# Sliding windows of an image batch: the iota behind four loads, copies in the band-crossing units, and the two final stores as one transfer each

## The chip, the cores and the metric

One core of one Trainium2 chip. The metric is the device time of one execution in microseconds; a lower number is better. Where two kernels are compared they ran on the same chip in alternation, and a ratio is the mean time of one kernel's fast runs over the mean of the other's fast runs of the same rounds, so it is not quite the ratio of the medians that are quoted.

## The reference

The batch is x of 16 images, 64 channels, 64 rows, 64 columns, float32 (16.8 MB). All windows of 8 by 8 at stride 4 are cut out, 15 by 15 of them an image, with all channels:

```python
for i in range(n_h):            # 15
    for j in range(n_w):        # 15
        h_start, w_start = i * stride, j * stride
        result[:, i, j] = x[:, :, h_start:h_start + 8, w_start:w_start + 8].copy()
```

The output has 3,600 windows of 64x8x8 floats, which is 3,600 contiguous rows of 16 KB, 59.0 MB. There is no arithmetic: the kernel loads, rearranges and stores.

## The kernel before

x lies in SBUF as a tile L of 128 partitions. Partition p = 64 ch + 4 b + q holds the channel half ch, image b and row band q (16 rows). A window needs both channel halves, so VectorE and ScalarE copy pieces of L into a gather tile G, in which one partition holds one whole window, 16 KB; G is then stored. There are four buffers G, used in turn.

The loads come from three queues. SyncE and GpSimd take eight partitions at a time:

```python
SMALL, HWP = 4, 8
def load(eng, ch, y, q, c0, c1):
    p0 = ch * HP + y * QP + q
    eng.dma_start(out=L[p0 : p0 + QP - HQ + 1 : HQ, c0:c1, :, :], in_=x_v[ch, y, q, :, c0:c1, :])

nc.gpsimd.iota(pi[:, :], ...)          # then some twenty 128x1 VectorE operations make the row indices
# ... cut ...
EC = 8
nc.scalar.dma_start(out=L[HP : HP + (B - 1) * HQ + 1 : HQ, 0:EC, :, :], in_=x_b[1, 0, :, 0:EC, :])
for y in range(NY):                    # 2
    for q in range(HQ):                # 4
        load(nc.sync, 0, y, q, SMALL, CL)            # hw is true for all eight
        load(nc.gpsimd, 0, y, q, 0, SMALL)
        load(nc.gpsimd, 1, y, q, EC if q == 0 else 0, CL)
```

A "plain" unit fills G with windows that lie inside one row band; its store has 128 rows. A "crossing" unit has, in one half of the partitions, windows that straddle two bands, so half of each piece comes through a stream shuffle from the next partition. The last band has no next one: 16 of the 128 rows get an index out of bounds and are not stored (the trace has 3,600 packets of 16 KB, one for each window). In a hi unit they lie in the upper 64 partitions, in a lo unit in the lower 64.

```python
def fill(g, half, s, j, lo, n, copies):
    # ... cut: the slices d, cols, f and cs ...
    for ch in (half, 1 - half):
        copy = copies[ch != half]
        if s < NSLOT - 1:
            copy(out=g[d, cs, :, :], in_=L[f, :, s * ST : s * ST + WS, cols])
        else:
            copy(out=g[d, cs, 0:ST, :], in_=L[f, :, s * ST : RB, cols])
            nc.vector.stream_shuffle(out=g[d, cs, ST:WS, :], in_=L[f, :, 0:ST, cols], mask=nxt)

act, dve = nc.scalar.copy, nc.vector.tensor_copy
def shf(out, in_):                       # a shuffle with the identity, which copies
    nc.vector.stream_shuffle(out=out, in_=in_, mask=same)
def mix(out, in_):                       # a quarter of the channels on ScalarE, the rest a shuffle
    k = out.shape[1] // 4
    act(out=out[:, 0:k], in_=in_[:, 0:k])
    shf(out=out[:, k:], in_=in_[:, k:])

def unit(j, s, fast=False):
    g = tile_()
    if s == 0:                           # plain
        fill(g, 0, 0, j, 0, HP, (act, dve if fast else shf))
        fill(g, 1, 1, j, 0, HP, (act, dve if fast else mix))
        scatter(g, idx, j, s)            # an indirect DMA issued by GpSimd
    else:                                # crossing
        turn = crossed % 2
        crossed += 1
        fill(g, turn, s, j, 0, HP, (act, act))
        fill(g, 1 - turn, s + 1, j, 0, HP, (shf, mix))
        scatter(g, (idx_hi, idx_lo)[turn], j, s)
```

In all there are 29 indirect stores: six of a `part` stage while the loads still run, then three fast plain units among them, then five groups of three crossing units and one plain unit. The last column of windows is not stored by index:

```python
j = NW - 1
tile_()                                  # skips one buffer
for s in range(2):
    g = tile_()
    # ... two copies on ScalarE, two on VectorE, 32x2048 each ...
    for q in range(HQ):                  # eight transfers of 256 KB in all
        free((nc.sync, nc.scalar)[s * q % 2].dma_start(out=o_q[q * NSLOT + s, j], in_=g_q[QP + q : QP + q + (B - 1) * HQ + 1 : HQ]))
```

Of the kernel before, what the change touches and what calls it, by code (L numbers as in the profile page):

```python
# [10 lines left out]
def kernel(  # L11
# [7 lines left out]
    nc = tc.nc  # L19
    P = nc.NUM_PARTITIONS  # L20

    B, C, H, W = x.shape
    Bo, NH, NW, Co, WSo, WSo2 = out.shape
    WS = int(window_size)
    ST = int(stride)
# [5 lines left out]
    CH = 2  # L31
    HQ = P // (B * CH)
    CL = C // CH
    RB = H // HQ
    NSLOT = RB // ST
    NWIN = NH * NW
    CFREE = C * WS * WS
    HP = P // CH
    YB = 8
    NY = B // YB  # L40
    QP = YB * HQ
# [7 lines left out]
    L = lpool.tile([P, CL, RB, W], f32)  # L49
# [4 lines left out]
# [5 lines that stand above are left out]
# [3 lines left out]
    def itile(name):  # L62
        return ipool.tile([P, 1], i32, name=name)

    pi, tb, tq, tc_, th, idx, idx_y0, idx_y1, idx_lo, idx_hi = (
        itile(n) for n in ("pi", "tb", "tq", "tc", "th", "idx", "idx_y0", "idx_y1", "idx_lo", "idx_hi")
    )
    FAR = float(2 * B * NWIN)
    nc.gpsimd.iota(pi[:, :], pattern=[[0, 1]], base=0, channel_multiplier=1)  # L69

    def bits(d, shift, mask):
        nc.vector.tensor_scalar(out=d[:, :], in0=pi[:, :], scalar1=shift, scalar2=mask, op0=ALU.logical_shift_right, op1=ALU.bitwise_and)  # L72
# [4 lines left out]
    def tt(d, a, b, op):  # L77
        nc.vector.tensor_tensor(out=d[:, :], in0=a[:, :], in1=b[:, :], op=op)  # L78
# [20 lines left out]
    tt(idx_lo, tb, th, ALU.add)  # L99
    mul(th, tc_, NW)  # L100
    tt(idx_lo, idx_lo, th, ALU.add)


    EC = 8
    x_b = x.rearrange("b (ch cl) (hq r) w -> ch hq b cl (r w)", ch=CH, hq=HQ)
    nc.scalar.dma_start(out=L[HP : HP + (B - 1) * HQ + 1 : HQ, 0:EC, :, :], in_=x_b[1, 0, :, 0:EC, :])

    for y in range(NY):
        for q in range(HQ):
            hw = y * HQ + q < HWP  # L110
            if hw:
                load(nc.sync, 0, y, q, SMALL, CL)
            load(nc.gpsimd, 0, y, q, 0, SMALL if hw else CL)
            load(nc.gpsimd, 1, y, q, EC if q == 0 else 0, CL)

    o_v = out.rearrange("b i j c r w -> (b i j) (c r w)")
    nxt = [min(p + 1, 31) for p in range(32)]
# [3 lines left out]
    o_q = out.rearrange("b i j c r w -> i j b (c r w)")  # L121

    def free(st):
        tc.declare_no_dep(st.ins, group="stores", reason="each store writes rows of its own")
        tc.add_to_no_dep_group("stores", st.ins)

    def scatter(g, ix, j, s):
        st = nc.gpsimd.indirect_dma_start(  # L128
            out=o_v,
            out_offset=bass.IndirectOffsetOnAxis(ap=ix[:, 0:1], axis=0),  # L130
            in_=g.rearrange("p c r w -> p (c r w)"),
            in_offset=None,
            element_offset=(s * NW + j) * CFREE,
            bounds_check=B * NWIN - 1,
            oob_is_err=False,
        )
        free(st)

    def fill(g, half, s, j, lo, n, copies):

        d = slice(half * HP + lo, half * HP + lo + n)
        cols = slice(j * ST, j * ST + WS)
        for ch in (half, 1 - half):
            f = slice(ch * HP + lo, ch * HP + lo + n)
            cs = slice(ch * CL, (ch + 1) * CL)
# [8 lines that stand above are left out]
    same = list(range(32))  # L154


    def shf(out, in_):
        nc.vector.stream_shuffle(out=out, in_=in_, mask=same)  # L158

    def mix(out, in_):  # L160
        k = out.shape[1] // 4
        act(out=out[:, 0:k], in_=in_[:, 0:k])  # L162
        shf(out=out[:, k:], in_=in_[:, k:])


    EARLY = 3
# [2 lines left out]
    def tile_():  # L169
        nonlocal at  # L170
        at += 1
        return G[(at - 1) % NG]
# [16 lines left out]
    def unit(j, s, fast=False):  # L189
        nonlocal crossed  # L190
        g = tile_()
        if s == 0:
            fill(g, 0, 0, j, 0, HP, (act, dve if fast else shf))
            fill(g, 1, 1, j, 0, HP, (act, dve if fast else mix))
            scatter(g, idx, j, s)
        else:

            turn = crossed % 2
            crossed += 1
            fill(g, turn, s, j, 0, HP, (act, act))  # L200
            fill(g, 1 - turn, s + 1, j, 0, HP, (shf, mix))
            scatter(g, (idx_hi, idx_lo)[turn], j, s)

    for n in range(EARLY):
# [3 lines left out]
    for n in range(EARLY):  # L208
        part(1, 2 * n)
        unit(*plain.pop(0), fast=True)  # L210
    while plain:
        for w in cross[:3]:
            unit(*w)
        cross = cross[3:]
        unit(*plain.pop(0))


    j = NW - 1
    tile_()
    for s in range(2):  # L220
        g = tile_()
        cols = slice(j * ST, j * ST + WS)
        for y in range(NY):
            d = slice(QP + y * QP, QP + (y + 1) * QP)
            for ch, copy in enumerate((act, dve)):
                f = slice(ch * HP + y * QP, ch * HP + (y + 1) * QP)
                copy(out=g[d, ch * CL : (ch + 1) * CL, :, :], in_=L[f, :, s * ST : s * ST + WS, cols])  # L227
        g_q = g.rearrange("p c r w -> p (c r w)")
        for q in range(HQ):
            free((nc.sync, nc.scalar)[s * q % 2].dma_start(out=o_q[q * NSLOT + s, j], in_=g_q[QP + q : QP + q + (B - 1) * HQ + 1 : HQ]))  # L230


# [33 lines left out]
```

## Time and profile before

| | before |
|---|---|
| time, median | 190.28 us (190.25 to 190.29), later 190.26 to 190.66 beside other kernels |
| span of the profiled run | 189.0 us (this run took 190.74 us, some 0.5 us over the median) |
| VectorE, ScalarE busy | 142.5 us, 139.2 us |
| mean rate of all transfers | 401 GB/s |
| last indirect store issued by GpSimd | 172.51 us |
| last plain stores issued | 181.44 to 182.86 us |

The prediction below shows the lines of the page, of the windows view and of the timeline that carry this. A window line reads: from and to, length, busy us of VectorE, ScalarE and GpSimd with their instruction counts, the clock, the DMA share (the mean share of 16 DMA engines with a packet in flight; it can pass 1: it is 1.03 from 8 to 28 us, where two queues load, and 1.00 to 1.01 from 52 to 172 us, under GpSimd's stores alone) and the rate.

The view by source line of the launch code has the columns line, engine, operation, count, shortest/median/longest in ns, first start and last start in us.

```profile
L261 POOLq DRAIN  x3: 51/105/12829, 172.3 to 188.7; - x3
```

GpSimd's queue drains for 12.8 us, from 172.3 to 185.1 us; GpSimd's last store has landed 1.89 us before the drain's end, at 183.23 us. In this kernel the drain's end is over 3.8 us before the span's end.

### The profile page before, as it was taken

The page shows a single profiled execution, that of the slowest core. Times are in us where ns is not written, and L with a number is a line of the kernel's source. Part 1 is how long each engine was busy: PE and PEld are TensorE (multiplying, and loading weights), DVE is VectorE, ACT ScalarE, POOL GpSimd, SP SyncE. Part 2 cuts the span into 40 slices and gives each one's busy share as a digit, 9 for nine tenths or more (in the row PEclk, how much of TensorE's full clock was granted, in tenths as well). Part 3 has the DMA queues.
Part 4 walks back from the last instruction along what each step waited for, and adds up shares of the span by engine and source line. Part 5 has one row for each costly group of instructions (what it writes and reads, how often), then busy time and mean ns, then how long its engine had stood idle before and what let it go on. Part 6 is the DMA issues. An engine that isn't in the chain of part 4 may idle for free.

```text
span 189.0 us, 557 instructions
## 1 busy us (share of the span) xinstructions
DVE 142.5 (75%) x200; ACT 139.2 (74%) x89; POOL 46.9 (25%) x50
## 2 busy tenths in 40 slices
DVE  4000009999697979799989999999999999997410
ACT  0000009998699999988889999999999999974740
POOL 7321212207217170522220222222222222223000
DMA  4999999999999999999999999999999999999993
GB/s 118 308 409 397 402 401 397 397 403 394 427 434 420 435 434 416 434 434 413 437 437 408 439 430 420 423 437 416 427 413 434 428 409 430 406 437 378 427 389 153
DMA packets 11044, 75.81 MB, mean 401 GB/s; under 512 B 3344, under 2 KB 3344, under 8 KB 7440
## 3 DMA queue, kind: packets, MB, share of 16 engines
q0 software_dynamic: 8784, 65.81, 84.0%
q1 hardware_dynamic: 2048, 8.91, 12.0%
q10 hardware_dynamic: 208, 1.05, 1.8%
q14 instruction: 4, 0.03, 0.0%
HBM read 16.78 MB, written 62.91 MB: 422 GB/s over the span
## 4 chain that ended last, share of the span: by engine, by line
DMA 66%; DVE 18%; issue 6%; ACT 3%; POOL 2%; DVEq 0%; ACTq 0%; PEldq 0%
DMA out_dram<-G,idx_hi 24%; DMA L<-in_x_dram 23%; DMA out_dram<-G,idx 13%; DVE G L158 10%; DMA out_dram<-G,idx_y 7%; DVE G L151 5%; DVE G L181 3%; ACT G L227 2%; POOL L L58 2%; ACT G L148 1%; DVE G L148 0%; DVEq L181 0%; POOL pi L69 0%; DVEq L158 0%; PEldq L261 0%
## 5 line engine op out<-in xcount | busy, mean ns | idle before, releaser
L148 ACT COPY G<-L 64x2048 f32<-64x2048 f32 x46 | 87.2, 1896 | 5.5 <-DMA out_dram<-G,idx 2.3
L181 DVE COPY G<-L 32x2048 f32<-32x2048 f32 x30 | 36.6, 1221 | 29.3 <-DMA L<-in_x_dram 26.7
L158 DVE STREAM_SHUFFLE G<-L 64x1024 f32<-64x1024 f32 (+3 forms) x40 | 55.7, 1392 | 1.3
L151 DVE STREAM_SHUFFLE G<-L 64x1024 f32<-64x1024 f32 x30 | 38.5, 1282 | 0.0
L181 ACT COPY G<-L 32x2048 f32<-32x2048 f32 x18 | 33.9, 1896 | 2.9 <-DMA L<-in_x_dram 2.3
L181 ACT ACT_TABLE_LOAD x1 | 1.3, 1283 | 28.3 <-DMA L<-in_x_dram 28.3
L58 POOL DMA_DIRECT2D L<-in_x_dram x16 | 10.9, 691 | 23.0 <-DMA L<-in_x_dram 22.5
L128 POOL DMA_INDIRECT out_dram<-G,idx_y x6 | 10.0, 1664 | 25.5 <-DVE G L181 24.5
L128 POOL DMA_INDIRECT out_dram<-G,idx x8 | 11.3, 1412 | 19.9 <-DVE G L158 6.5
L128 POOL DMA_INDIRECT out_dram<-G,idx_hi x8 | 7.7, 963 | 30.7 <-DVE G L151 23.1
L128 POOL DMA_INDIRECT out_dram<-G,idx_lo x7 | 6.7, 961 | 27.5 <-DVE G L151 19.1
L227 ACT COPY G<-L 32x2048 f32<-32x2048 f32 x4 | 7.6, 1896 | 5.1 <-DMA out_dram<-G,idx_lo 4.0
L162 ACT COPY G<-L 64x256 f32<-64x256 f32 (+1 forms) x20 | 9.1, 456 | 0.5
L227 DVE COPY G<-L 32x2048 f32<-32x2048 f32 x4 | 4.9, 1219 | 3.5 <-DMA out_dram<-G,idx_hi 2.4
L148 DVE COPY G<-L 64x2048 f32<-64x2048 f32 x6 | 7.3, 1222 | 0.2
L158 DVE LOAD_MASK_SELECT G<-L x40 | 0.4, 9 | 2.1 <-DMA out_dram<-G,idx_y 1.2
L72 DVE TENSOR_SCALAR tb<-pi 128x1 int32<-128x1 int32 x1 | 0.2, 153 | 1.0 <-POOL pi L69 1.0
L78 DVE TENSOR_TENSOR th<-tc,tq 128x1 int32<-128x1 int32 x2 | 0.3, 156 | 0.0
L75 DVE TENSOR_SCALAR th<-tc 128x1 int32<-128x1 int32 x2 | 0.3, 154 | 0.0
L69 POOL IOTA pi<- 128x1 int32 x1 | 0.1, 124 | 0.4 <-PEq L261 0.4
L151 DVE LOAD_MASK_SELECT G<-L x30 | 0.2, 7 | 0.0
L78 DVE CUSTOM_DVE_ANT_0 idx_lo<-tb,th 128x2 uint16<-128x2 uint16 x1 | 0.2, 159 | 0.0
(18 smaller groups left out, 2.6 us busy)
## 6 DMA issues: line engine op xcount, KB each, us to landing
L<-in_x_dram SPq DMA_DIRECT2D x8, 896.0 KB
L<-in_x_dram POOLq DMA_DIRECT2D x6, 1024.0 KB, 21.6
L<-in_x_dram POOLq DMA_DIRECT2D x2, 768.0 KB, 18.3
out_dram<-G SPq DMA_DIRECT2D x6, 256.0 KB
L<-in_x_dram POOLq DMA_DIRECT2D x8, 128.0 KB, 21.6
L<-in_x_dram ACTq DMA_DIRECT2D x1, 512.0 KB
out_dram<-G ACTq DMA_DIRECT2D x2, 256.0 KB
out_dram<-G,idx POOLq DMA_INDIRECT x8, 12.3
```

The lines of the kernel that those rows point to most:

```text
L58: eng.dma_start(out=L[p0 : p0 + QP - HQ + 1 : HQ, c0:c1, :, :], in_=x_v[ch, y, q, :, c0:c1, :])
L69: nc.gpsimd.iota(pi[:, :], pattern=[[0, 1]], base=0, channel_multiplier=1)
L72: nc.vector.tensor_scalar(out=d[:, :], in0=pi[:, :], scalar1=shift, scalar2=mask, op0=ALU.logical_shift_right, op1=ALU.bitwise_and)
L75: nc.vector.tensor_scalar(out=d[:, :], in0=a[:, :], scalar1=float(m), scalar2=None, op0=ALU.mult)
L78: nc.vector.tensor_tensor(out=d[:, :], in0=a[:, :], in1=b[:, :], op=op)
L128: st = nc.gpsimd.indirect_dma_start(out=o_v, out_offset=bass.IndirectOffsetOnAxis(ap=ix[:, 0:1], axis=0), in_=g.rearrange("p c r w -> p (c ...
L148: copy(out=g[d, cs, :, :], in_=L[f, :, s * ST : s * ST + WS, cols])
L151: nc.vector.stream_shuffle(out=g[d, cs, ST:WS, :], in_=L[f, :, 0:ST, cols], mask=nxt)
L158: nc.vector.stream_shuffle(out=out, in_=in_, mask=same)
L162: act(out=out[:, 0:k], in_=in_[:, 0:k])
L181: (act if (2 * d + ch) % 3 == 0 else dve)(out=g[d * QP : (d + 1) * QP, ch * CL : (ch + 1) * CL, :, :], in_=L[f : f + QP, :, s * ST : s * S ...
L227: copy(out=g[d, ch * CL : (ch + 1) * CL, :, :], in_=L[f, :, s * ST : s * ST + WS, cols])
```

## The change

The intent: GpSimd starts its loads earlier; VectorE, which looks full, gets faster copies for two of four shuffles in each crossing unit (a copy of a 64x2048 piece takes 1222 ns in the kernel before, a shuffle 2428 ns); the last two tiles go out earlier, in one transfer each.

```diff
-    nc.gpsimd.iota(pi[:, :], pattern=[[0, 1]], base=0, channel_multiplier=1)
+    # (the loads stand here now, and in their loop:)
+            if y == 0 and q == 1:
+                nc.gpsimd.iota(pi[:, :], pattern=[[0, 1]], base=0, channel_multiplier=1)
@@ helpers
-    def mix(out, in_):
+    def mix(out, in_, rest=shf):
         k = out.shape[1] // 4
         act(out=out[:, 0:k], in_=in_[:, 0:k])
-        shf(out=out[:, k:], in_=in_[:, k:])
+        rest(out=out[:, k:], in_=in_[:, k:])
+    def mixc(out, in_):
+        mix(out, in_, dve)
@@ crossing unit
-            fill(g, 1 - turn, s + 1, j, 0, HP, (shf, mix))
+            fill(g, 1 - turn, s + 1, j, 0, HP, (dve, mixc))
@@ last column
-    tile_()
     for s in range(2):
         g = tile_()
-        # four copies of 32x2048, two on each engine
+        # ScalarE: 32x2048 and 32x1024; VectorE: 32x2048 twice and 32x1024
-        for q in range(HQ):
-            free((nc.sync, nc.scalar)[s * q % 2].dma_start(out=o_q[q * NSLOT + s, j], in_=g_q[...]))
+        g_q = g.rearrange("p c r w -> p (c r w)")[QP : QP + B * HQ]
+        free(nc.sync.dma_start(out=o_q[s::NSLOT, j].rearrange("q b f -> b q f"), in_=g_q))
```

More of the change, by code (lines that the diff above doesn't have):

```diff
@@ L68 @@
     FAR = float(2 * B * NWIN)
-    nc.gpsimd.iota(pi[:, :], pattern=[[0, 1]], base=0, channel_multiplier=1)
+    EC = 8
+    x_b = x.rearrange("b (ch cl) (hq r) w -> ch hq b cl (r w)", ch=CH, hq=HQ)
+    nc.scalar.dma_start(out=L[HP : HP + (B - 1) * HQ + 1 : HQ, 0:EC, :, :], in_=x_b[1, 0, :, 0:EC, :])
+    for y in range(NY):
+        for q in range(HQ):
+            hw = y * HQ + q < HWP
+            if hw:
+                load(nc.sync, 0, y, q, SMALL, CL)
+            load(nc.gpsimd, 0, y, q, 0, SMALL if hw else CL)
+            load(nc.gpsimd, 1, y, q, EC if q == 0 else 0, CL)
+            if y == 0 and q == 1:
+                nc.gpsimd.iota(pi[:, :], pattern=[[0, 1]], base=0, channel_multiplier=1)
     def bits(d, shift, mask):
@@ L101 @@
     tt(idx_lo, idx_lo, th, ALU.add)
-    EC = 8
-    x_b = x.rearrange("b (ch cl) (hq r) w -> ch hq b cl (r w)", ch=CH, hq=HQ)
-    nc.scalar.dma_start(out=L[HP : HP + (B - 1) * HQ + 1 : HQ, 0:EC, :, :], in_=x_b[1, 0, :, 0:EC, :])
-    for y in range(NY):
-        for q in range(HQ):
-            hw = y * HQ + q < HWP
-            if hw:
-                load(nc.sync, 0, y, q, SMALL, CL)
-            load(nc.gpsimd, 0, y, q, 0, SMALL if hw else CL)
-            load(nc.gpsimd, 1, y, q, EC if q == 0 else 0, CL)
     o_v = out.rearrange("b i j c r w -> (b i j) (c r w)")
@@ L218 @@
     j = NW - 1
-    tile_()
+    half_c = CL // 2
     for s in range(2):
@@ L222 @@
         cols = slice(j * ST, j * ST + WS)
-        for y in range(NY):
-            d = slice(QP + y * QP, QP + (y + 1) * QP)
-            for ch, copy in enumerate((act, dve)):
-                f = slice(ch * HP + y * QP, ch * HP + (y + 1) * QP)
-                copy(out=g[d, ch * CL : (ch + 1) * CL, :, :], in_=L[f, :, s * ST : s * ST + WS, cols])
-        g_q = g.rearrange("p c r w -> p (c r w)")
-        for q in range(HQ):
-            free((nc.sync, nc.scalar)[s * q % 2].dma_start(out=o_q[q * NSLOT + s, j], in_=g_q[QP + q : QP + q + (B - 1) * HQ + 1 : HQ]))
+        for y, ch, c0, c1, copy in (
+            (0, 0, 0, CL, act),
+            (0, 1, 0, CL, dve),
+            (1, 0, 0, half_c, act),
+            (1, 1, 0, CL, dve),
+            (1, 0, half_c, CL, dve),
+        ):
+            d = slice(QP + y * QP, QP + (y + 1) * QP)
+            f = slice(ch * HP + y * QP, ch * HP + (y + 1) * QP)
+            copy(
+                out=g[d, ch * CL + c0 : ch * CL + c1, :, :],
+                in_=L[f, c0:c1, s * ST : s * ST + WS, cols],
+            )
+        g_q = g.rearrange("p c r w -> p (c r w)")[QP : QP + B * HQ]
+        free(nc.sync.dma_start(out=o_q[s::NSLOT, j].rearrange("q b f -> b q f"), in_=g_q))
 _INS = ['x', 'window_size', 'stride']
```

## The prediction

> **What bounds the kernel now.** I read the page first, its 40 slices above all, then the windows view by stage, then the timeline of the end. Of the page:
>
> ```profile
> span 189.0 us, 557 instructions
> DVE 142.5 (75%) x200; ACT 139.2 (74%) x89; POOL 46.9 (25%) x50
> ...
> DVE  4000009999697979799989999999999999997410
> ACT  0000009998699999988889999999999999974740
> ...
> DMA  4999999999999999999999999999999999999993
> GB/s 118 308 409 397 402 401 397 397 403 394 427 434 420 435 434 416 434 434 413 437 437 408 439 430 420 423 437 416 427 413 434 428 409 430 406 437 378 427 389 153
> ...
> q0 software_dynamic: 8784, 65.81, 84.0%
> q1 hardware_dynamic: 2048, 8.91, 12.0%
> ```
>
> Each slice is 4.7 us. VectorE and ScalarE look full in the second half, and so do the DMA engines, from the second slice to the last but one. Which of them limits is decided by the windows view (busy us of DVE, ACT, POOL; clock; DMA share; GB/s):
>
> ```profile
> 8.00:28.00 20.00, 0.00 (x0) 0.00 (x0) 3.58 (x6) 1.00 1.03 399
> ...
> 52.00:84.00 32.00, 28.30 (x29) 30.61 (x18) 11.86 (x7) 1.00 1.01 429
> 84.00:100.00 16.00, 14.99 (x23) 13.76 (x11) 3.43 (x4) 1.00 1.01 427
> 100.00:120.00 20.00, 19.70 (x33) 19.27 (x15) 3.85 (x4) 1.00 1.00 425
> ...
> 160.00:172.00 12.00, 11.56 (x17) 8.59 (x6) 1.92 (x2) 1.00 1.00 421
> 172.00:178.00 6.00, 2.83 (x3) 4.20 (x3) 1.58 (x1) 1.00 0.92 388
> 178.00:184.00 6.00, 2.04 (x2) 3.38 (x2) 0.00 (x0) 1.00 0.98 412
> 184.00:189.00 5.00, 0.00 (x0) 0.00 (x0) 0.00 (x0) 1.00 0.37 154
> ```
>
> From 8 to 172 us the DMA share stays at 1.00 or above, and 421 to 429 GB/s is what full DMA engines give for the stores. So the kernel is **bound by the DMA engines** for 164 of its 189 us. Capacity is lost in two places only: before 8 us, and from 172 us on.
>
> VectorE is nonetheless the slowest feeder. In a band-crossing unit its four shuffles take from one 64x768 shuffle at 155.69 to the next at 160.44 us, 4.75 us a unit; ScalarE needs about 4.27 us (its 64x256 copies start at 159.56 and 163.83). The unit's store is 112 rows of 16 KB, 1.835 MB, which takes 4.3 us at 425 GB/s. VectorE therefore falls behind, but behind it lies a backlog of stores: the first band-crossing store (83.59 us) takes 14.0 us to land, the last (168.17 us) 9.3 us. The backlog shrinks by about 5 us without running dry. At the end it shows:
>
> ```profile
> 168.17 0.96 POOL L128 DMA_INDIRECT out_dram<-G,idx_hi  x1 [3.80 <-ACT G L148]
> ...
> 172.51 1.58 POOL L128 DMA_INDIRECT out_dram<-G,idx  x1 [3.38 <-issue]
> 172.70 3.81 ACT L227 COPY G<-L 32x2048 f32<-32x2048 f32 x2 [3.99 <-DMA out_dram<-G,idx_lo]
> ...
> 176.54 7.58 SPq L230 DMA_DIRECT2D out_dram<-G  x6
> 177.59 3.81 ACT L227 COPY G<-L 32x2048 f32<-32x2048 f32 x2 [1.07 <-DMA out_dram<-G,idx_hi]
> ...
> 181.44 2.19 ACTq L230 DMA_DIRECT2D out_dram<-G  x2
> ```
>
> The last full unit is stored only at 172.51 us. ScalarE idles 3.99 us, because the first plain tile waits for a buffer whose store was issued at 163.41 us, and the second for the one issued at 168.17 us. The last 1 MB is not issued before 181.44 us; bytes stop near 187 us and the span ends at 189.0 us.
>
> [...] the indirect issue takes 0.96 us beside shuffles and up to 2.50 us beside copies. [...]the trace's long stretches hold 421 to 429, slices peak at 439. [...]here about 2 us lie between the last bytes and the span's end. No choice in the change touches those 2 us.
>
> **The change part by part.**
>
> 1. *Iota behind four loads.* Now the iota runs at 0.84 us and GpSimd's first load is issued at 1.48 us, 0.64 us later. Behind the change it can be issued near 0.85 us; loads five to eight stay where they were. The index arithmetic ends some 2 to 3 us later than 3.6 us, but its first user is the store at 43.3 us. The hardware queue starts at 0.74 us anyhow, and the DMA share from 2 to 3 us is 0.65 and about 0.9 from 4 to 6, so only part of 0.64 us becomes bytes: I take **-0.3 us** (0.1 to 0.6).
>
> 2. *Copies in band-crossing units.* Per unit one 64x1024 shuffle (1283 ns) and one 64x768 shuffle (999 ns) become copies. An estimate from the 1222 ns of a 64x2048 copy, with about 160 ns fixed (the small index operations take 143 to 159)[...]: 160+531=691 ns and 160+398=558 ns. Saved: 0.59+0.44=1.03 us a unit, 15.5 us of VectorE time in 15 units. A unit then costs VectorE about 3.7 us, and ScalarE (4.27) becomes the slower engine. On the path this is worth almost nothing directly. Three crossing units and one plain unit move 3x1.835+2.097=7.60 MB, 17.9 us at 425 GB/s; ScalarE needs 3x4.27+4.46=17.3 us, VectorE before 3x4.75+4.3=18.5 us, after 15.4 us. So VectorE, the slowest before, drops out, and the DMA engines stay the bound. What is gained is that the backlog is not eaten: the rate may stay near 427 instead of drifting to 421 (85 us x 0.5% = **-0.4 us**), and the last unit is issued earlier.[...]
>
> 3. *Final stores.* The skipped tile goes. The first plain tile takes the buffer stored at 158.66 us, the second the one stored at 163.41 us (free at 172.6 us), each one unit earlier. ScalarE gives one half-copy of four to VectorE: 1.90+0.95=2.85 us against 2x1.22+0.70=3.1 us for a tile, instead of 3.81 us. The second tile should be copied by about 176 us and its single 1 MB store issued then, 5.4 us ahead of 181.44, with some 9 us of stores still in the queues. So the last bytes are limited by bandwidth, not by issue. The windows from 172 us carry 6x0.388+6x0.412+5x0.154=5.57 MB, 13.0 us at 427 GB/s, ending at 185.0 instead of about 186.8 us. There are eight hi and seven lo stores, which skip 16 rows in opposite halves, so I leave 0.4 us for unequal engines: **-1.4 us**. Eight transfers becoming two removes issues that cost 0.57 to 1.60 us each, off the path once issued early.
>
> Sum: -0.3-0.4-1.4 = **-2.1 us**; that makes 188.2 us. As a refilled queue may do a little better than I credit, I put it at 187.9 us.
>
> **The rivals.** (a) *VectorE was the bound of the middle.* For it: 99% busy from 100 to 160 us, and a chain of waits that runs through shuffles for many us there. Then the middle would run at ScalarE's 17.3 us a cycle instead of 18.5, 5 cycles, -6 us, and the time would be near 182 to 183 us. Against it: a DMA share of 1.00 throughout; moving 7.60 MB in 17.3 us would be 439 GB/s, which only single slices reach. (b) [...]stores start late and the engines run dry. For it: issues of up to 2.50 us in the stage of 52 to 84 us. Against it: that same stage, full of copies, has the best rate of all, 429 GB/s. If true, 190 to 191 us. (c) *One large hardware transfer feeds too slowly,* or competes with the last indirect store, so that the end is as late as before: then parts 1 and 2 alone, some 189.5 us. Against it: a hardware load of 896 KB is issued in as little as 677 ns, and both queues share the same engines, so order matters little.
>
> **Range and chances.** Bandwidth gives a floor: the 42.9 MB that the windows carry from 84 us on would take 98.2 us at the 437 GB/s of the best slices instead of 100.5 us at 427; that is 2.3 us more gain, so 185.6 us. The pessimistic rivals give 189.5 to 190. I take 185.7 to 189.6 us. Faster by over 2% means below 186.5 us, in the outer part of the optimistic side: 0.16. Slower by over 2%[...]: 0.01. Within 2%: 0.83.
>
> **What would show each step right or wrong.** Right: GpSimd's first load near 0.85 us; copies of about 0.69 and 0.56 us and VectorE's busy time down by some 15 us; ScalarE the engine with least idle time in the middle; landing times that stay at 11 to 14 us rather than shrink to 9; DMA share still 1.00 with 425 to 429 GB/s; the last store issued before 178 us; and no window below 400 GB/s until about 184 us. Wrong: a middle at 435 or more (rival a), a DMA share under 0.95 beside copies (b), or a low-rate tail of several us after the last issue (c).

In part 2 the estimate stands on the trace alone: the 1222 ns of the copy less 160 ns is 1062 ns for 2048 elements, so 531 ns for 1024 and 398 ns for 768. The rates, issue times and the 2 us in the paragraph before the parts are measured, and so is the pair of 1222 ns for a 64x2048 copy and 2428 ns for the shuffle. Rival (b) is that copies on VectorE delay GpSimd's issue of the stores; how they might was cut from it, and from the chances. The engines that rival (c) has both queues share show in the packets in flight in the changed kernel: from 178 to 182 us a mean of 5.26 of GpSimd and 10.85 of SyncE, 16.1 together, where GpSimd's stores alone have 16.1 from 52 to 84 us.

## The result

The changed kernel takes **192.47 us** (192.28 to 192.71, 4 runs) against 190.26 us (190.11 to 190.29): a ratio of 1.0113, 95% interval 1.0098 to 1.0128. It is 1.1% slower, where a gain of 1.3% had been predicted.

The page of the changed kernel:

```profile
span 190.7 us, 522 instructions
...
DVE 129.1 (68%) x172; ACT 137.5 (72%) x89; POOL 48.2 (25%) x50
...
DVE  0300019997897969877789779979977989588000
...
DMA  4999999999999999999999999999999999999970
GB/s 120 329 405 401 397 402 396 401 398 409 440 419 431 433 433 402 436 436 416 430 433 418 424 440 426 416 430 433 412 419 436 416 412 431 416 423 412 433 302 31
```

VectorE is freed as planned: 13.4 us less busy. The two new copies are as fast as worked out, in the view of groups by form:

```profile
L151 DVE COPY G<-L 64x1024 f32<-64x1024 f32 x15 | 10.3, 688 | 7.7 <-DMA out_dram<-G,idx_hi 2.5 <-DMA out_dram<-G,idx_y 1.9 <-ACT G L164 1.9
L165 DVE COPY G<-L 64x768 f32<-64x768 f32 x15 | 8.3, 555 | 0.5
```

The DMA engines do not gain from it. The windows of the changed kernel:

```profile
84.00:100.00 16.00, 13.14 (x18) 13.94 (x11) 3.29 (x3) 1.00 1.00 425
...
160.00:172.00 12.00, 9.19 (x10) 10.27 (x8) 3.51 (x3) 1.00 1.00 421
172.00:178.00 6.00, 4.05 (x5) 3.67 (x3) 0.37 (x1) 1.00 1.02 429
178.00:184.00 6.00, 0.00 (x0) 0.00 (x0) 0.00 (x0) 1.00 0.93 396
184.00:191.00 7.00, 0.00 (x0) 0.00 (x0) 0.00 (x0) 1.00 0.18 77
```

The middle is as before. From 172 to 178 us the refilled queue does what was hoped, 429 in place of 388 GB/s. What it wins is then lost, because the end has two parts nobody asked for. The first is in finer windows of the end:

```profile
183.00:184.00 1.00, 0.00 (x0) 0.00 (x0) 0.00 (x0) 1.00 0.62 262
184.00:185.00 1.00, 0.00 (x0) 0.00 (x0) 0.00 (x0) 1.00 0.46 197
185.00:186.00 1.00, 0.00 (x0) 0.00 (x0) 0.00 (x0) 1.00 0.46 197
186.00:187.00 1.00, 0.00 (x0) 0.00 (x0) 0.00 (x0) 1.00 0.35 147
```

The same stretches of the kernel before:

```profile
183.00:184.00 1.00, 0.00 (x0) 0.00 (x0) 0.00 (x0) 1.00 0.82 344
184.00:185.00 1.00, 0.00 (x0) 0.00 (x0) 0.00 (x0) 1.00 0.83 344
185.00:186.00 1.00, 0.00 (x0) 0.00 (x0) 0.00 (x0) 1.00 0.74 311
186.00:187.00 1.00, 0.00 (x0) 0.00 (x0) 0.00 (x0) 1.00 0.28 115
```

In the changed kernel, from 184 to 187 us, no more than half of the DMA engines have work. Counting the packets in flight in the trace gives 8.0 of 16 from 184 to 186 us. The other eight were done near 183.5 us.

The second is after the last byte. Packets end at 187.0 us before and at 187.5 us after, but the span ends at 189.0 and 190.7 us. The timeline of the end and GpSimd's drain of the changed kernel:

```profile
170.12 2.25 POOL L129 DMA_INDIRECT out_dram<-G,idx  x1 [5.21 <-ACT G L164]
173.04 4.20 SPq L242 DMA_DIRECT2D out_dram<-G  x2
```

```profile
L273 POOLq DRAIN  x3: 51/105/20000, 169.9 to 190.4; - x3
```

Both plain stores are issued by 177.2 us, 5 us earlier than before, as planned. But GpSimd's drain now lasts 20.0 us, to 189.9 us, and the end of the program waits for it.

**The two halves, store by store.** Each store leaves sixteen completion records in the trace. They are read here as one for each of the sixteen DMA engines; they carry no engine numbers, but they fall into eight early and eight late ones (50.65 to 51.41 and 52.73 to 53.65 us for the first store of the kernel before). The table (worked out from these records, us from the span's start) gives the median of the early and of the late eight for the first indirect store and for the 28th, the last crossing one; then the last landing of a GpSimd store and of a hardware store, the end of GpSimd's drain and of the span:

```
kernel       store 1        store 28         last landing        drain    span
             early  late    early   late     GpSimd   hardware   end      end
before       50.73  53.13   174.69  177.29   183.23   187.61     185.12   188.96
after        50.31  53.05   173.84  177.39   188.01   187.83     189.90   190.69
```

The late eight are 2.4 to 2.7 us behind from the start of the stores. After store 28 the late half still has, if the rows spread evenly, sixteen rows of 16 KB an engine to store, 8 of the last indirect store and 4 of each plain one; at 0.612 us a row that is 9.8 us. Before: 177.29+9.8=187.1 us, and the late eight of its last plain transfer land at a median of 187.13 us. So the late half had **no idle time at the end even before the change**; all that idled there was the early half. After: 177.39+9.8=187.2 us, and the late eight of the last plain store land at a median of 187.17 us.

Two theories follow. **H**: the late half carries more bytes and sets the end. Which engines a transfer uses was assumption, since the traces have no engine numbers: that each SyncE load, of eight partitions, runs on the same half of the engines, the small GpSimd loads on that half too, and the large ones on the other. The trace of the kernel before agrees as far as it can. SyncE's loads have a median of 8 packets in flight from 8 to 28 us, and never over 9, where ScalarE's load of sixteen partitions has a mean of 15.5 from 3 to 4 us; the first SyncE load leaves one completion record at 2.13 us and eight single ones from 10.34 to 11.29 us, ScalarE's load sixteen from 5.24 to 5.73 us. On the assumption one half loads 8x0.918 MB from SyncE and 8x0.131 MB of small GpSimd transfers, 8.39 MB, and the other the large GpSimd ones, 6x1.049+2x0.786=7.86 MB. The difference of 0.52 MB is four rows of 16 KB an engine, 2.4 us, and the gap at the first store is 2.4 us. That the late half is the one of SyncE's loads shows in the spacing too: the eight completions of the last SyncE load come 0, 0.04, 0.20, 0.26, 0.58, 0.71, 0.76 and 0.95 us after the first of them, the late eight of the first store 0, 0.03, 0.20, 0.23, 0.57, 0.69, 0.81 and 0.92 us, while of the early eight six come within 0.11 us and two 0.7 us later. The sixteen rows that a hi store leaves out are read as two an engine of the early half, those of a lo store as two of the late half (in the kernel before the gap grows by 1.1 to 1.3 us at each hi store and shrinks by 1.2 to 1.4 us at each lo one); with eight hi and seven lo stores the late half has two more, six rows or 3.7 us in all (at store 28 the gap is 2.6 us before and 3.6 us after the change). **D**: GpSimd's drain ends 1.89 us after the last landing of a GpSimd store in both kernels (183.23 to 185.12, 188.01 to 189.90), and 0.8 us later the span ends. Before, where a hardware store lands last, the span ends 1.35 us after the landing. So an indirect store that lands last costs 1.3 us more, and the drain can still end last, by less, where a hardware store lands up to some 1.3 us after it.

The rivals: **P**, the copies delay GpSimd's issues and so slow the store stream (in the kernel before an indirect issue takes 0.96 us beside shuffles and up to 2.50 us beside copies; in the changed kernel the issues of crossing units take 0.97 to 1.36 us); the large transfers are slow; and the iota.

### The profile page after: what moved, and what is told of

It is laid out like the page before. It is cut to its first block, busy times and chain, and to the rows that moved or that the text cites. A ratio compares the mean times of both kernels' runs of the same rounds, so it can differ in the third digit from the quotient of the medians.

```text
span 190.7 us, 522 instructions
## 1 busy us (share of the span) xinstructions
DVE 129.1 (68%) x172; ACT 137.5 (72%) x89; POOL 48.2 (25%) x50
## 4 chain that ended last, share of the span: by engine, by line
DMA 71%; ACT 9%; DVE 8%; POOL 2%; issue 2%; DVEq 1%; ACTq 0%; POOLq 0%; PEldq 0%
DMA out_dram<-G,idx_hi 28%; DMA L<-in_x_dram 22%; DMA out_dram<-G,idx 7%; DMA out_dram<-G,idx_lo 7%; DMA out_dram<-G,idx_y 7%; ACT G L149 5%; ACT G L186 3%; DVE G L186 3%; DVE G L152 2%; POOL L L58 2%; DVE G L151 1%; DVE G L237 1%; DVEq L273 1%; DVE G L165 1%; ACT G L164 0%
## 5 line engine op out<-in xcount | busy, mean ns | idle before, releaser
L186 DVE COPY G<-L 32x2048 f32<-32x2048 f32 x30 | 36.7, 1225 | 26.3 <-DMA L<-in_x_dram 23.0
L186 ACT COPY G<-L 32x2048 f32<-32x2048 f32 x18 | 33.9, 1895 | 3.6 <-DMA L<-in_x_dram 2.4
L160 DVE STREAM_SHUFFLE G<-L 64x2048 f32<-64x2048 f32 (+1 forms) x10 | 21.6, 2161 | 0.2
L58 POOL DMA_DIRECT2D L<-in_x_dram x16 | 10.9, 692 | 22.8 <-DMA L<-in_x_dram 21.8
L151 DVE COPY G<-L 64x1024 f32<-64x1024 f32 x15 | 10.3, 688 | 7.7 <-DMA out_dram<-G,idx_hi 2.5
L129 POOL DMA_INDIRECT out_dram<-G,idx_hi x8 | 8.7, 1093 | 25.7 <-ACT G L164 25.7
L165 DVE COPY G<-L 64x768 f32<-64x768 f32 x15 | 8.3, 555 | 0.5
L149 DVE COPY G<-L 64x2048 f32<-64x2048 f32 x6 | 7.3, 1222 | 0.2
L237 DVE COPY G<-L 32x2048 f32<-32x2048 f32 (+1 forms) x6 | 6.2, 1041 | 1.0 <-DMA out_dram<-G,idx_lo 0.5
L237 ACT COPY G<-L 32x2048 f32<-32x2048 f32 (+1 forms) x4 | 5.9, 1470 | 1.1 <-DMA out_dram<-G,idx_lo 0.7
## 6 DMA issues: line engine op xcount, KB each, us to landing
out_dram<-G,idx_hi POOLq DMA_INDIRECT x8, 13.5
```

The source lines that it names most:

```text
L129: st = nc.gpsimd.indirect_dma_start(out=o_v, out_offset=bass.IndirectOffsetOnAxis(ap=ix[:, 0:1], axis=0), in_=g.rearrange("p c r w -> p (c ...
L165: rest(out=out[:, k:], in_=in_[:, k:])
L186: (act if (2 * d + ch) % 3 == 0 else dve)(out=g[d * QP : (d + 1) * QP, ch * CL : (ch + 1) * CL, :, :], in_=L[f : f + QP, :, s * ST : s * S ...
L237: copy(out=g[d, ch * CL + c0 : ch * CL + c1, :, :], in_=L[f, c0:c1, s * ST : s * ST + WS, cols],)
```

## The experiments

All results were correct but for one, which is marked. Each run is compared with the kernel before in the same rounds.

### One part at a time

Three kernels take one part of the change each into the kernel before; the fourth is the changed kernel with `(shf, mix)` in place of `(dve, mixc)`.

> The kernel before with the iota moved behind four loads, nothing else. Theory H[...]: the head start of GpSimd's loads goes to the other eight engines, so 190.0 to 190.4 us. Rival (the head start counts in full): 189.6 to 189.8 us.

Measured 190.57 us (190.52 to 190.73), ratio 1.0016 (0.9999 to 1.0033). No gain, and just above the expected 190.4. But the head start itself did not come. GpSimd's loads in the kernel before and in the changed kernel (in `d1_iota` the first is at 1.38 us too):

```profile
1.48 4.99 POOL L58 DMA_DIRECT2D L<-in_x_dram  x8 [0.52 <-issue]
```

```profile
1.38 2.63 POOL L58 DMA_DIRECT2D L<-in_x_dram  x4 [0.93 <-PEq L273]
```

The first load is issued 0.10 us earlier, not 0.64 us: the iota took 0.12 us, and most of the wait before the first load is there without it too. The first store lands at 53.17 us in the late half (53.13 before) and at 50.66 us in the early one (50.73). So this run says nothing on what a real head start would be worth.

> The kernel before with the copies in the band-crossing units, nothing else. Theory H: VectorE was not the bound, the last stores still go out on the hardware queues and land last, so 189.9 to 190.6 us. Rival P (copies [...]slow the stream of indirect stores): 191.5 us or more. Rival V (VectorE was the bound of the middle): 188 us or less.

Measured 191.2 us (190.83 to 191.43), ratio 1.0041 (1.0024 to 1.0057). Slower than theory H had it, less than P had it: VectorE was not the bound, and the edit has a cost that neither number covers.

> The kernel before with the new final stores (two transfers, next two tiles), shuffles kept. Theory H: the hardware stores share the engines with the last indirect store, which lands last; GpSimd's drain then ends 1.9 us after it and sets the end: 191.5 to 192.6 us. Rival P: 190.3 us or less, since no copy was added.

Measured 190.84 us (190.3 to 191.0), ratio 1.0031 (1.0014 to 1.0048). This missed H and D as then stated: with shuffles the last landing is a hardware store's at 187.15 us, and the indirect one's at 185.84 us comes 1.3 us before it. The drain still ends last, at 187.73 us, but only 0.14 us after SyncE is through with its own waits. The new stores alone, one 1 MB transfer in place of four of 256 KB and issued earlier, gain nothing and lose some 0.6 us at most.

> The changed kernel with the shuffles put back (iota and final stores stay changed). Theory H: 191.5 to 192.6 us, no better than the changed kernel by more than 0.7 us. Rival P (the copies cost the time): 190.3 us or less.

Measured 190.31 us (190.23 to 190.99), ratio 1.0011 (0.9991 to 1.0032). The expectation of H failed here and that of P came true. So **the edit that brings the copies carries the loss, and most of it only together with the new stores**: some 2 us beside them (2.2 in medians, 1.9 by the ratios), 0.8 us or so alone. Its trace: last landings 185.80 us (GpSimd) and 187.03 us (hardware), drain to 187.69 us, span 188.49 us. Its drain line:

```profile
L273 POOLq DRAIN  x3: 51/105/15529, 172.2 to 188.2; - x3
```

Against this the changed kernel lands last 0.98 us later, and ends 2.68 in place of 1.46 us after that, which is 1.22 us more. The drain ends last in both kernels, but here only 0.21 us after SyncE is through (187.48 us), in the changed kernel 1.40 us (188.50 us). Read by the drain alone: the last GpSimd landing is 2.21 us later, and so is the span's end (2.20 us).

### The drain

`h_last` stores the last full unit by two SyncE transfers:

```diff
+            if hw:
+                for h in range(2):
+                    g_h = g.rearrange("p c r w -> p (c r w)")[h * HP : (h + 1) * HP]
+                    free(nc.sync.dma_start(out=o_q[h::NSLOT, j].rearrange("q b f -> b q f"), in_=g_h))
+            else:
                 scatter(g, idx, j, s)
```

> The changed kernel, with the last full unit stored by two hardware transfers from SyncE in place of GpSimd's indirect store; same bytes, same buffers, same order. Theory D (in the changed kernel the last store to land is an indirect one, and GpSimd's drain ends 1.9 us after it): the drain ends well before the end, the span ends 1.4 us after the last landing in place of 2.7 us, 191.0 to 191.5 us. Rival (only the bytes count): 192.3 to 192.7 us.

Measured 194.72 us, ratio 1.0223 (1.0202 to 1.0244): a miss. The drain part behaved, the drain ended 3.5 us before the span, which ended 1.1 us after the last landing (191.82 us). But each new transfer reads 64 partitions of one half of SBUF, and the windows view shows engines that are busy and slow:

```profile
172.00:178.00 6.00, 1.90 (x3) 1.74 (x2) 0.00 (x0) 1.00 0.99 270
```

The hardware packets of 16 KB took a median of 1.19 us there, against 0.61 us elsewhere. The plain stores of the changed kernel, which read partitions 32 to 95, do not have this fault (a median of 0.614 us). Why the packets are slow there is not shown. So two cleaner tests of D were made. `e_skip` puts the skipped `tile_()` back, so the plain stores go out later. `g_shuffles` is the changed kernel with shuffles, with the very last store on GpSimd:

```diff
-        free(nc.sync.dma_start(out=o_q[s::NSLOT, j]...
+        free((nc.sync, nc.gpsimd)[s].dma_start(out=o_q[s::NSLOT, j]...
```

> The changed kernel with the skipped tile put back, so that its two final stores use the buffers of the kernel before and are issued later, the last near 182 us; copies, iota and single transfers stay. Theory D (GpSimd's drain after the last indirect store adds 1.2 us): a hardware store lands last, bytes end as before, 190.9 to 191.6 us. Rival (issuing the last stores early helps, or costs nothing): 192.4 us or more.

Measured 191.0 us (190.79 to 191.15), ratio 1.0033: 1.5 us faster than the changed kernel in medians, by issuing the last stores later.

> The changed kernel with shuffles (190.31 us), its very last store issued by GpSimd in place of SyncE, same bytes. Theory D: the last landing is then one of GpSimd's queue and the drain adds about 1.2 us: 191.2 to 191.9 us. Rival: 190.0 to 190.6 us.

Measured 191.75 us (191.65 to 192.01), ratio 1.0068: 1.4 us slower than 190.31 (1.1 us by the ratios, since the two ran in different rounds), with the same bytes. The drain lines of the two, `e_skip` first:

```profile
L274 POOLq DRAIN  x3: 51/105/16797, 169.8 to 188.7; - x3
```

```profile
L273 POOLq DRAIN  x3: 46/111/10478, 179.0 to 190.0; - x3
```

The first ends at 186.6 us, well before the last hardware landing at 187.79 us; the span ends at 189.0. The second ends at 189.45 us, 1.93 us after the last landing (187.52 us, a GpSimd store); the span ends at 190.2. D holds both ways. Over all traces the drain ends 1.85 to 1.93 us after the last GpSimd landing.

### The halves

`b_even` takes 12 channels of the q = 0 loads from SyncE and gives them to one ScalarE transfer over 16 partitions; `bh_both` adds `h_last`, and `b_before` is the edit in the kernel before.

```diff
+    E0 = 12
+    nc.scalar.dma_start(out=L[0 : (B - 1) * HQ + 1 : HQ, CL - E0 : CL, :, :], in_=x_b[0, 0, :, CL - E0 : CL, :])
-                load(nc.sync, 0, y, q, SMALL, CL)
+                load(nc.sync, 0, y, q, SMALL, CL - E0 if q == 0 else CL)
```

> The changed kernel with 12 channels of the first row group's loads, 0.79 MB, taken from the SyncE loads[...] and given to one ScalarE transfer[...]; same bytes in all. Theory H[...]: the half that lands late comes 1.3 to 2.0 us earlier, the stretch with eight active engines at the end goes, 190.4 to 191.3 us. Rival ([...]halves don't matter): 192.2 to 192.7 us.

> Both edits in one: even loads and the last unit by hardware transfers. Theories H and D together: 189.0 to 190.1 us, below the kernel before. If only one holds: 190.4 to 191.5 us.

> The kernel before with the even loads. Theory H: 188.6 to 189.4 us; the kernel before had the same eight engines as its limit. Rival (VectorE or the issue of the last stores limits the kernel before): 190.0 to 190.5 us.

Measured 195.6, 197.37 and 193.73 us (ratios 1.0272, 1.0360, 1.0174): all far off, and as tests of H confounded. The edit did even out the start: in `b_even` the halves of the first store land at 53.66 and 53.73 us. But the transfer also brings rows of the second batch half ahead of those that the first copies need, and the loads and first stores of `b_even` are slower:

```profile
8.00:28.00 20.00, 0.00 (x0) 0.00 (x0) 2.92 (x5) 1.00 1.03 387
44.00:52.00 8.00, 7.85 (x7) 7.93 (x6) 4.61 (x3) 1.00 0.95 361
```

The loads ran at 387 in place of 400 GB/s in the changed kernel, the first indirect store was issued at 46.33 in place of 42.79 us, and from 44 to 52 us the DMA share was 0.95 in place of 1.05. Later one half fell behind again, to a gap of 3.2 us at store 28 (177.18 and 180.34 us), more than the bytes explain: from the ninth store to the 28th it took 86.6 us (86.4 in `b_before`), against 85.4 us in the changed kernel and 85.0 us in the kernel before for the same bytes. Why it does so after an even start was not tried, and H does not explain it.

A better tool needs no other timing: the number of hi and lo stores. `turn = 1 - crossed % 2` makes the first crossing unit a lo one, so that there are seven hi and eight lo stores. By the reading above it moves two rows an engine, 2x0.61=1.2 us, from the late half to the early one, and nothing else.

> The changed kernel with the first band-crossing unit a lo one in place of a hi one, so seven hi and eight lo stores instead of eight and seven[...]. Theory H (the half that lands late sets the end): about 2x0.61=1.2 us less, 191.0 to 191.6 us. Rival (only the sum of bytes counts, or the end is set by something else): 192.2 to 192.7 us.

Measured 190.01 us (189.76 to 190.22), ratio 0.9982 (0.9960 to 1.0004): 2.5 us faster than the changed kernel, and faster than either theory expected. Packets end at 186.2 in place of 187.5 us, 1.3 us earlier, as H has it; and the last landing is again a hardware store's (186.51 us; GpSimd's is at 185.30), so most of the drain's cost goes too:

```profile
L273 POOLq DRAIN  x3: 51/105/17437, 169.8 to 187.7; - x3
```

It ends at 187.19 us, still last, but 0.23 us after SyncE is through (186.96 us) in place of 1.40 us.

> The same swap in the kernel before. Theory H: 188.9 to 189.6 us. Rival (the late issue of the last stores limits it): 190.1 to 190.5 us.

Measured 189.58 us (189.34 to 189.69), ratio 0.9953 (0.9932 to 0.9974): 0.8 us less, somewhat short of the 1.2 us expected. The dose was then widened, with ten and with six hi stores of fifteen (`turn = int(crossed % 3 == 2)` and `turn = int(crossed % 5 not in (1, 3))`):

> The kernel before with ten hi and five lo stores in place of eight and seven, the same bytes in all. Theory H: [...]4x0.61=2.4 us, so 192.2 to 193.0 us. Rival (the halves don't matter): 190.0 to 190.6 us.

Measured 192.72 us (192.62 to 192.74), ratio 1.0117 (1.0100 to 1.0134): 2.2 us slower in medians of the same rounds, where bytes say 2.4 (four rows an engine more for the late half).

> The kernel before with six hi and nine lo stores. [...]no further gain over seven hi stores (189.58 us), 189.2 to 190.3 us. Rival (each lo store in place of a hi one simply saves 0.8 us): 188.8 us.

Measured 189.69 us (189.3 to 190.05), ratio 0.9953 (0.9930 to 0.9976): no further gain, so the turning point lies about where the bytes put it (by the same sum the half that was late now has two rows an engine, 1.2 us, less than the other). With the sum of bytes the same and only the order of hi and lo units changed, these runs **show that one half of the DMA engines set the end, in the kernel before as well**. Which engines make up that half is not shown, since the trace has no engine numbers.

### What the copies do

`x_half` keeps VectorE's time short without any copy: each of the two new copies becomes a shuffle of half the elements. Its output is wrong, which doesn't matter for the time.

```diff
+    def shh(out, in_):
+        h = out.shape[1] // 2
+        shf(out=out[:, 0:h], in_=in_[:, 0:h])
-            fill(g, 1 - turn, s + 1, j, 0, HP, (dve, mixc))     # mixc: rest = dve
+            fill(g, 1 - turn, s + 1, j, 0, HP, (shh, mixc))     # mixc: rest = shh
```

> The changed kernel with each of its two new copies replaced by a shuffle of half the elements (a wrong result on purpose): VectorE takes about as long as with copies[...]. Theory T (the earlier issue alone costs the time): 191.8 to 192.7 us. Theory P (the copies themselves): 190.0 to 190.8 us. In between: both, or the instruction fetch, which here falls where the shuffles had it.

Measured 192.28 us (192.13 to 192.37), ratio 1.0087: within 0.2 us of the changed kernel in medians, 0.5 us less by the ratios (1.0113), and far from the 1.0011 of `u2_shuffles`. **About three quarters of the loss or more need no copy; they come with VectorE being done earlier.** The rest, 0.5 us at most, is not told from the spread between rounds. The last indirect issue and the plain stores, in the timelines of `x_half` and of `u2_shuffles`:

```profile
169.77 2.20 POOL L129 DMA_INDIRECT out_dram<-G,idx  x1 [3.51 <-ACT G L164]
...
172.65 4.21 SPq L246 DMA_DIRECT2D out_dram<-G  x2
```

```profile
172.39 1.85 POOL L129 DMA_INDIRECT out_dram<-G,idx  x1 [3.38 <-ACT G L237]
...
174.91 3.76 SPq L242 DMA_DIRECT2D out_dram<-G  x2
```

Everything is issued 2.3 to 2.6 us earlier, into engines of which the late half is already full. In `x_half` the last GpSimd landing is then at 187.85 us and the last hardware one at 187.67 us, with the drain to 189.74 us; with shuffles they are 185.80, 187.03 and 187.69 us. The plain stores are in flight beside the last indirect store for longer (in the changed kernel a mean of 5.3 packets of GpSimd and 10.9 of SyncE from 178 to 182 us, in the kernel before 11.1 and 4.8), and the indirect store lands last; `e_skip`, with the same copies and later plain stores, has that landing at 184.75 us.

There is a second, smaller effect. From the ninth store, the last before the crossing units, to the 28th the late half takes 84.92 to 85.10 us in five kernels with shuffles, and 85.39 to 85.93 us in the five with a fast VectorE whose halves have the same bytes; the early half takes 84.49 to 84.84 and 84.05 to 84.12 us. Earlier issue keeps the early half busier, and the late half loses about 0.5 us. It may be the cost of `d2_copies` as well, whose late half is 0.3 us behind the kernel before at store 28 and whose packets end 0.9 us later. What the halves share there is not shown by any run.

Last, a detail of the traces looked like a cause. VectorE's instruction fetches (one packet of 8 KB each) fell at 146 us with shuffles and at 160 us with copies, and in the changed kernel one late engine was 1.4 us behind the median of its half at store 28, against 0.2 to 0.6 us with shuffles. `f_shift` adds sixty tiny copies on VectorE while it waits for the loads, to move the fetch:

```diff
+    spare = itile("spare")
+    for _ in range(60):
+        nc.vector.tensor_copy(out=spare[:, :], in_=idx[:, :])
```

> The changed kernel with 60 tiny VectorE copies of 128x1 added while VectorE waits for the loads, which cost no time but move the later instruction fetches of VectorE's queue by 60 instructions. Theory F (the fetch at 160 us leaves one engine of the late half about 1 us behind, and its indirect rows land last): the fetch moves to near 120 us, the last landing comes 0.4 to 1.2 us earlier, 191.2 to 192.1 us. Rival (the fetch does not matter): 192.3 to 192.7 us.

Measured 193.06 us (192.66 to 193.27), ratio 1.0127. The fetch moved to 119.4 us and nothing got better; the straggler was still 1.3 us behind. That idea is dropped; in `x_half` the fetch is at 146 us as well, and the time does not care, and in `e_skip` it is at 160 us with a straggler of only 0.6 us. What makes one engine straggle stays open.

### A version below both

> The changed kernel with shuffles and a lo unit first: iota and final stores as changed, no copies. If the halves set the end and a hardware store still lands last: 1.2 us less than 190.3, so 188.9 to 189.5 us, below the kernel before and t7_before. If the indirect store lands last: 190 us or more.

Measured 189.56 us (189.26 to 189.87), ratio 0.9946 (0.9929 to 0.9963). With `t7_before` (0.9953) it is the best, half a per cent below the kernel before; the two are not told apart. One changed line, `turn = 1 - crossed % 2`, gains 0.8 us, a third of the 2.4 us that the whole change was meant to gain. (In `t7_shuffles` the drain still ends last, by 0.15 us.)

## Why the prediction was wrong, point by point

- **The bound.** "bound by the DMA engines" was right, and rival (a), VectorE, rightly refused: VectorE gave up 13.4 us, the rates of the middle stayed at 420 to 428 GB/s. But a share of 1.00 is a mean over sixteen engines. The step that failed is "Capacity is lost in two places only", with its sequel in part 3, "the last bytes are limited by bandwidth, not by issue": the capacity lost after 172 us belonged to the half that was done, and the other half, full until 187.0 us, had nothing to win.
- **Part 1**, -0.3 us. Measured alone, 1.0016, no gain. The step that failed is "Behind the change it can be issued near 0.85 us": the first load came at 1.38 in place of 1.48 us, a head start of 0.10 and not 0.64 us. The reading put the whole wait down to the iota, which took 0.12 us of it.
- **Part 2**, -0.4 us. The durations (688 and 555 against 691 and 558 ns) and the saving of 1.03 us a unit were right. The effect on time had the wrong sign: alone 1.0041, and some 2 us beside the new stores. "What is gained is that the backlog is not eaten" came true (a hi store took a median of 13.5 us to land in place of 11.1 us) but was worth nothing, since the late half had hardly run out of work. Rival (b), slower issues beside copies, is not the main reason either, by `x_half`.
- **Part 3**, -1.4 us. This is the term with the largest error. 5.57 MB at 427 GB/s assumed that any engine may carry them; "I leave 0.4 us for unequal engines" should have been 3.7 us between the halves by bytes; the late one then ends 1.8 us after an even share would, which is all of the 1.8 us hoped for. The last packets ended at 187.5 us, not at 185.0 plus 0.4.
- **The end.** "No choice in the change touches those 2 us" failed: 1.35 us after the last landing before, 2.68 us after, since it matters which queue lands last. (Of those 2 us 0.6 lie between the last packet and the last landing before, 0.5 us after.) Rival (c) had the form nearest to this, that hardware stores compete with the last indirect store, but dismissed it with "order matters little". The order was worth 1.5 us in `e_skip`, and the queue of the very last store 1.1 to 1.4 us in `g_shuffles`.
- **The range.** The 187.9 us lie 0.3 us beyond the sum of the parts, with no working. The rivals that were considered ended at 191 us; none had a cost at the end that grows when stores are issued earlier.
- **In sum**: the changed kernel against the one with shuffles is 0.98 us of later landing and 1.22 us of drain (or, as the drain ends last in both, a last GpSimd landing that is 2.21 us later), in the profiled spans 190.69-188.49=2.20 us, and 2.16 us in the medians of their own rounds (1.9 us by the ratios).

## What to carry to other kernels

When the DMA engines are full on average, look at the sixteen completions of single stores: if they fall into an early and a late group, bytes taken from the late group may shorten the kernel where faster issue does not, as here. At the end of a program with stores from several queues, see which queue lands last; a GpSimd store there is followed by the drain of its queue, which ended 1.85 to 1.93 us after its landing here, 0.8 us before the span where it was last, and which can end last even when a hardware store lands a little later (in `t7_after` it still ends last, by 0.23 us, with that store's landing 1.2 us later). Issue as early as possible is no aim in itself: here a slower VectorE gave the better end.
